# Neighbourhood heads: border keys by one transposition, meta keys by one product on diagonal blocks

## The chip, the cores and the metric

The kernel runs on one core of a Trainium2 chip. The time is that of the device for one execution, in microseconds. Engines are named as in the profile: PE (TensorE), ACT (ScalarE), DVE (VectorE), POOL (GpSimd), SP (SyncE, which issues nearly all DMAs).

## The reference

Two encoder layers over 512 grid tokens (8 rows of 64 columns) and 16 meta tokens, 1024 features, all in float32. Each layer projects the normed tokens into 42 chunks of 128 columns, runs two kinds of attention with 8 heads of 64, gates, projects and merges the results, and adds them to the residual. The part that matters here is the neighbourhood branch:

```python
s_mm = einsum('bqhd,bmhd->bhqm', qm, km) * scale                # meta queries see the meta keys alone
o_meta = einsum('bhqm,bmhd->bqhd', softmax(s_mm), vm)
...
s_win = einsum('bchd,bicjhd->bhcij', q_row, k_win) * scale      # a window of 8 rows x 16 columns
s_win = s_win + bias[None]
s_meta = einsum('bchd,bmhd->bhcm', q_row, km) * scale           # and the 16 meta keys
p = softmax(concatenate([s_win, s_meta], axis=-1))
return einsum('bhcij,bicjhd->bchd', p_win, v_win) + einsum('bhcm,bmhd->bchd', p_meta, vm)
```

## The kernel before, in words

**Precision.** A float32 operand x of a product is kept as a high part (x rounded to the matmul format F32R) and a low part (x minus the high part). Projections are three products per block of 128 rows: high by high, high by low, low by high (`product`, lines 387 to 397; tiles `whi`, `wlo` for weights, `hh`, `hl` for tokens). The helper `split` (lines 255 to 260) makes both parts from a bank of PSUM: ACT copies the high part, DVE subtracts. Weights come by DMA as `raw`, ACT casts them to `whi` (L306) and POOL subtracts for `wlo` (L307), three halves of a chunk ahead of their product. For the neighbourhood branch a product's 128 output rows are the 64 features by the high part of the values and the 64 features by their low part; `combine` adds the two halves (an ACT copy, then a DVE addition).

**Order of the work.** TensorE runs the projections without a break; attention is hung between them. After every half or whole chunk a `tick` runs what is due, for the neighbourhood heads (`side_na`) and for the other branch's heads (`side_gqa`; tiles S, av). A head's six stages (`windowed_head`, line 1029) are due 0, 2, 4, 5, 5 and 7 ticks after its start: load the bias, scores, transposes 1, 2 and 3, sums. The next head starts four ticks later at the earliest. The values of a pair of heads are transposed 3 and 4 ticks after the first head's start (`values`, `window_edges`). Each engine takes its instructions in one order, made by the scheduler from these places and from the table `BEHIND`, which names pairs of instructions of one engine that must follow each other (the n-th writer of a tile behind the m-th writer of another).

**One head.** Tokens stand column by column, so that 128 queries are 16 grid columns, and block b of queries needs a stretch of keys: 208, 272, 272 and 208 columns of an array of 544 (`BLK`), which holds the 512 keys and the 16 metas twice, behind key 63 and ahead of key 448. The four blocks of scores are two products each (Sb: keys' high and low parts). DVE adds the bias and takes the maximum (L1062), ACT takes the exponential into the bias tile (L1064). Then the weights of 128 keys are turned so that keys lie on partitions, by TensorE transpositions against an identity:

- ta (`transposes1`): four pieces of 128 keys; split into `tah`, `tal` of 512 columns.
- tb (`transposes2`): two pieces of 128 keys, and the two borders, each 64 border keys with 16 metas, 80 columns (block 0 to the left, block 3 to the right); split into `tbh`, `tbl`.
- tc (`transposes3`): 64 columns around the metas of blocks 1 and 2; a mask `inner` zeroes what isn't meta; the high parts go to rows 0 to 63 and the low parts to rows 64 to 127 of `na`, 256 columns (L864, L870).

`sums` (avb, L1124) is eleven products into one bank of 512 columns: one for `na` (256 columns), four for `tah` and `tal` and two for `tbh` and `tbl` (256), and four of 80 rows by 128 columns for the borders.

In layer 0 alone (`full`) the 16 meta queries have a softmax of their own: two products of 16 columns (sm), a transposition of a padded 128x32 tile (tm), a split by DVE into the padded tile `mm`, and a product of 16 columns (avbm).

The values tile `VB2` has six slots: 0 to 2 for inner keys, 3 and 4 for the borders with their metas (80 rows), 5 for the metas of blocks 1 and 2. `window_edges` fills 3 to 5 by three transpositions of 80 columns (vtc).

Of the kernel before, what the change touches and what calls it, by code (L numbers as in the profile page):

```python
# [18 lines left out]
P = 128  # L19
# [4 lines left out]
NMETA = 16  # L24
# [34 lines left out]
BLK = ((0, 0, 208), (480, 64, 272), (208, 208, 272), (752, 336, 208))  # L59
# [3 lines left out]
BLK_META = 448  # L63
# [10 lines left out]
    ),  # L74
    "DVE": (
# [7 lines left out]
    ),  # L83
# [12 lines left out]
    ),  # L96
    "Pool": (
        ("KB1_20", 0, "za1_0", 0), ("ga0", 7, "wlo0_24_0", 0), ("ga0", 51, "wlo1_36_1", 0), ("ga0", 52, "wlo1_36_1", 0),
        ("wl6KB", 1, "gb0", 0), ("wlo0_21_0", 0, "ga0", 10), ("wlo1_38_1", 0, "zb1_3", 0),
    ),  # L100
# [58 lines left out]
def trunk_kernel(ctx: ExitStack, tc: tile.TileContext, xT, w, gn, gf, bias, rope, out):  # L159
# [72 lines left out]
    for kind, (cols, n, dt) in {"ga": (256, 1, F32R), "na": (256, 1, F32R), "mm": (NMETA, 1, F32R), "pm": (32, 1, F32), "inv": (32, 1, F32)}.items():  # L232
# [9 lines left out]
    inner = cpool.tile([P, 1], F32, name="inner")  # L242
    nc.gpsimd.memset(inner, 1.0)
    nc.gpsimd.affine_select(inner, inner, pattern=[[0, 1]], compare_op=ALU.is_ge, fill=0.0, base=-NMETA, channel_multiplier=1)
    nc.gpsimd.affine_select(inner, inner, pattern=[[0, 1]], compare_op=ALU.is_ge, fill=0.0, base=3 * NMETA - 1, channel_multiplier=-1)

# [278 lines left out]
    for l in range(DEPTH):  # L525
# [74 lines left out]
        def stack_k(tag, name, k, n, eng):  # L600
# [6 lines left out]
            return [(t[:, 0], t[:, 1]) for t in (one, two_)]  # L607
# [85 lines left out]
        def pair_factors(t, c, n, name):  # L693

            f = slot("G", f"pf{name}{l}") if n > 1 else tiny.tile([P, P], F32, tag="pf", bufs=1, name=f"pf{name}{l}")
# [82 lines left out]
        def window_scaled(c, name):  # L778

            t, e = slots.tile([P, NKEY], F32, tag="E", bufs=BUFS["E"], name=name), HD + 2 * NMETA  # L780
            for ps, a, b in project(c, True):
                r = rbc[:, a:b]
                if a == 0:
                    nc.vector.tensor_mul(t[:, :HD], ps[:, :HD], r[:, :HD])
                    nc.vector.tensor_mul(t[:, e + HD:e + b], ps[:, HD:], r[:, HD:])
                else:
                    i, j = NREAL - HD - a, NREAL - a
                    nc.vector.tensor_mul(t[:, e + a:], ps[:, :i], r[:, :i])
                    nc.vector.tensor_mul(t[:, e:e + HD], ps[:, i:j], r[:, i:j])
                    nc.vector.tensor_mul(t[:, HD:e].rearrange("p (i t) -> p i t", i=2),  # L790
                                         ps[:, j:].unsqueeze(1).to_broadcast([P, 2, NMETA]),
                                         r[:, j:].unsqueeze(1).to_broadcast([P, 2, NMETA]))
            return t
# [13 lines left out]
        def window_edges(v, out, name):  # L807

            ps = bank(ps_t, f"vt{name}", "tp")
            for i, a in enumerate((0, EDGE, HD - NMETA)):  # L810
                nc.tensor.transpose(ps[:EDGE, P * i:P * (i + 1)], v[:, a:a + EDGE], ident)
            split(out[:EDGE, 3:, :, 0], out[:EDGE, 3:, :, 1], ps[:EDGE, :3 * P].rearrange("p (t h d) -> p t h d", t=3, h=2))
            nc.scalar.copy(out[HD:, 5], out[:HD, 5].bitcast(F32))
# [23 lines left out]
        def combine(tag, o, hh, av, c0, n):  # L837

            r, q = rows(hh)
            t = slot(tag, f"cmb{nc.next_id()}")  # L840
# [547 lines left out]
```

## Time and profile before

| what | value |
|---|---|
| median of 3 timed runs | 819.68 us (819.6 to 820.24) |
| the profiled execution's own time | 818.64 us |
| its span, first to last instruction | 816.7 us |
| granted clock of TensorE | 0.999 |
| neighbourhood heads | 16, eight in each layer |
| ta, tb, tc, tm, vtc transpositions | 64, 64, 16, 8, 24 |
| avb, sm, avbm products | 176, 16, 8 |

In the profile a row of a group has line, engine, operation, output and inputs, shapes, count, then the busy time, the mean of one in ns and the idle time of the engine ahead of them with what ended it. A row of the timeline has start and duration in us. A matmul's duration holds its latency, which overlaps the next one's, so durations of neighbours add up to more than the time between their starts. PEld is the loading of stationary weights, which runs beside the matmuls. A few matmul records can be missing.

### The profile page before, as it was taken

The numbers are of one execution on the slowest core, as the hardware profiler recorded it, in microseconds if no ns is written. First come the engines' busy times: TensorE is split into PE (matmuls) and PEld (weight loads), VectorE is DVE, ScalarE is ACT, GpSimd is POOL, SyncE is SP. The second block draws the span as 40 slices with busy tenths as digits, with TensorE's granted clock in tenths as the row PEclk, the third lists the DMA queues.
The fourth block names the chain that finished last, engine by engine and source line by source line (L and its number), as shares of the span: only waits on it lengthen the run. The fifth ranks groups of instructions, "written<-read, shape, count | busy, mean of one in ns | idle before, by whom it ended". The sixth has DMA issues, their size and how long they took to land.

```text
span 816.7 us, 16071 instructions
## 1 busy us (share of the span) xinstructions
PE 808.8 (99%) x5658; PEld 755.1 (92%) x5658; DVE 505.2 (62%) x1154; ACT 473.5 (58%) x1137; POOL 418.0 (51%) x362
## 2 busy tenths in 40 slices
PE   9999999999999999999999999999999999999997
PEld 9999999999999999999988989998988888888786
DVE  7566767796785662365547666676867655324733
ACT  8645777677865654443445557666758755544322
POOL 1654454454554544655754645554625555556651
PEclk9999999999999999999999999999999999999999
DMA  8347474667645563435555575766775555652602
GB/s 299 108 133 216 145 212 131 183 212 204 184 146 183 159 210 119 142 105 173 153 122 137 141 231 154 213 162 179 194 227 159 171 181 152 198 174 90 206 1 104
DMA packets 113248, 134.99 MB, mean 165 GB/s; under 512 B 31888, under 2 KB 66192, under 8 KB 113168
## 3 DMA queue, kind: packets, MB, share of 16 engines
q1 hardware_dynamic: 112448, 132.90, 54.9%
q8 instruction: 45, 0.74, 0.4%
q10 hardware_dynamic: 720, 1.06, 0.4%
q14 instruction: 35, 0.29, 0.1%
HBM read 98.50 MB, written 21.84 MB: 147 GB/s over the span
## 4 chain that ended last, share of the span: by engine, by line
PE 94%; DMA 2%; ACT 1%; DVE 1%; issue 1%; SPq 1%; POOLq 0%; POOL 0%; DVEq 0%; ACTq 0%
PE pp L393 20%; PE pp L391 20%; PE pp L392 20%; PE av L977 4%; PE y L393 4%; PE y L391 4%; PE y L392 4%; PE avb L1124 2%; PE S L627 2%; PE S L628 2%; PE pf L1306 2%; PE pf L1308 2%; PE pf L1307 2%; PE pp L516 2%; DMA raw<-in_w_dram 1%; PE Sb L628 1%
## 5 line engine op out<-in xcount | busy, mean ns | idle before, releaser
L307 POOL TENSOR_TENSOR wlo<-raw,whi 128x512 fp32r<-128x512 f32 x210 | 284.4, 1364 | 287.1 <-ACT whi L306 223.3
L391 PE MATMUL pp<-hh,whi 128*128 128x256 f32 (+2 forms) x1040 | 325.2, 313 | 0.0
L393 PE MATMUL pp<-hh,wlo 128*128 128x256 f32 (+2 forms) x1040 | 324.1, 312 | 0.0
L392 PE MATMUL pp<-hl,whi 128*128 128x256 f32 (+2 forms) x1040 | 323.4, 311 | 0.0
L393 PEld LDWEIGHTS pp<-hh,wlo 128*128 128x128 f32 x1040 | 195.7, 188 | 10.3
L392 PEld LDWEIGHTS pp<-hl,whi 128*128 128x128 f32 x1040 | 195.7, 188 | 9.3
L391 PEld LDWEIGHTS pp<-hh,whi 128*128 128x128 f32 x1040 | 195.9, 188 | 8.7
L306 ACT CAST whi<-raw 128x512 fp32r<-128x512 f32 x210 | 128.0, 619 | 106.3 <-PE pp L392 36.2
L970 POOL TENSOR_TENSOR ga<-pm,ga 32x128 fp32r<-32x128 f32 x64 | 39.4, 615 | 64.1 <-ACT ga L968 39.9
L939 DVE STREAM_TRANSPOSE P<-P 128x512 f32<-128x512 f32 x64 | 46.5, 727 | 29.8 <-ACT P L913 29.4
L1203 DVE TENSOR_TENSOR mg<-pp,rbc 128x256 f32<-128x256 f32 (+2 forms) x48 | 24.8, 516 | 54.0 <-PE pp L393 53.7
L909 DVE CUSTOM_DVE_ANT_0 P<-S,r 128x528 f32<-128x528 f32 x64 | 44.8, 701 | 15.5 <-PE S L628 14.7
L260 DVE TENSOR_TENSOR ptl<-P,pth 128x512 fp32r<-128x512 f32 x64 | 48.9, 780 | 4.7 <-ACT pth L259 4.2
L913 ACT ACTIVATE P<-P,st 128x528 f32<-128x528 f32 x64 | 47.2, 737 | 1.7
L1064 ACT ACTIVATE bias<-bias,stb 128x208 f32<-128x208 f32 (+1 forms) x64 | 31.0, 485 | 18.2 <-DVE stb L1062 18.2
L1204 ACT ACTIVATE mg<-mg 128x256 f32<-128x256 f32 (+2 forms) x48 | 23.6, 492 | 28.0 <-DVE mg L1203 27.9
L259 ACT CAST pth<-P 128x512 fp32r<-128x512 f32 x64 | 39.3, 614 | 0.9 <-DMA P<-turn 0.8
L392 PE MATMUL pp<-mx,whi 128*128 128x272 f32 (+1 forms) x128 | 36.4, 285 | 0.0
L391 PE MATMUL pp<-mx,whi 128*128 128x272 f32 (+1 forms) x128 | 36.4, 285 | 0.0
L393 PE MATMUL pp<-mx,wlo 128*128 128x272 f32 (+1 forms) x128 | 36.4, 285 | 0.0
L912 ACT ACTIVATE st<-st 128x1 f32<-128x1 f32 x64 | 12.9, 202 | 40.4 <-DVE st L909 40.1
L977 PE MATMUL av<-pth,VA 128*128 128x256 f32 x128 | 34.0, 289 | 0.0
(534 smaller groups left out, 1717.9 us busy)
## 6 DMA issues: line engine op xcount, KB each, us to landing
raw<-in_w_dram SPq DMA_DIRECT2D x210, 256.0 KB
turn<-P SPq DMA_DIRECT2D x32, 528.0 KB
P<-turn SPq DMA_DIRECT2D x128, 128.0 KB
bias<-in_bias_dram SPq DMA_DIRECT2D x16, 480.0 KB
KB<-KB SPq DMA_DIRECT2D x24, 272.0 KB
rawl<-in_w_dram SPq DMA_DIRECT2D x16, 256.0 KB
x<-in_xT_dram SPq DMA_DIRECT2D x8, 264.0 KB
xr<-in_xT_dram SPq DMA_DIRECT2D x8, 264.0 KB
```

The lines of the kernel that those rows point to most:

```text
L259: split_at["hi"] = nc.scalar.copy(hi, src)
L260: split_at["any"] = nc.vector.tensor_sub(lo, src, hi.bitcast(F32))
L306: cast = nc.scalar.copy(hi, raw)
L307: sub = nc.gpsimd.tensor_sub(lo, raw, hi.bitcast(F32))
L391: nc.tensor.matmul(ps, wh, rh[:, a:b], start=i == 0, stop=False)
L392: nc.tensor.matmul(ps, wh, rl[:, a:b], start=False, stop=False)
L393: nc.tensor.matmul(ps, wl, rh[:, a:b], start=False, stop=i == n - 1)
L909: newest["max"] = nc.vector.tensor_tensor_reduce(p[:n], joined(S)[:n], scale[:n].to_broadcast([n, NTOK]), 1.0, -3e38, ALU.mult, ALU.max, s ...
L913: nc.scalar.activation(p[:n], p[:n], AF.Exp, bias=st[:n, 1:2], scale=1.0, accum_out=st[:n, 2:3] if total is None else total)
L939: nc.vector.transpose(c["both"][:n, a:b], c["both"][:n, a:b])
L970: nc.gpsimd.tensor_sub(tm[64 + 32 * t:96 + 32 * t, n * t:n * (t + 1)], m, tm[:32, :n].bitcast(F32))
L977: nc.tensor.matmul(c["av"], rows2(c["t"][i][0]), c["t"][i][1], start=i == 0, stop=i == 8)
```

## The change: what it does

All of it is in the neighbourhood heads, their values, and the table.

- **Borders.** The four blocks change places in the bias tile (`BLK`), so that the last 64 keys of block 3 and the first 64 of block 0 lie side by side at column 416 (`ENDS`). One transposition of 128 columns turns both. From each, ACT copies the high part to its own 64 rows of a tile `ne`, and DVE writes the low part to the other 64 rows; one product contracts over both, 128 rows by 128 columns, against a values slot that holds the same 64 values twice.
- **Metas.** POOL copies the metas of all four blocks, each twice, into a tile `nm` of 128 columns; one transposition (tc) turns them. ACT multiplies by `sign` (minus one for the first 16 of every 32 rows, plus one for the others) into `nh`, rounded; DVE forms tp * `second` - `nh`, which is the high part in the first 16 rows and the low part in the others, and writes the 32 rows of a block to its own 128 columns of `na`, now 128x512. One product of 512 columns, against values that repeat the metas eight times, covers the metas of all four blocks. It is the seventh of nine products.
- **Meta queries (layer 0).** One sm product of 32 columns (the keys' high and low parts side by side), added by ACT and DVE; the probabilities are stored twice in a 16x32 tile, whose transposition moves 16 columns in the tc bank; avbm contracts over 32 rows.
- **Values.** `window_edges` does two transpositions of 128 columns; three copies and three subtractions fill the slots, two copies double the borders. `window_scaled` writes the metas to a tile of their own.
- **The table** `BEHIND` has 119 pairs; two of its lines are shown.

```diff
-BLK = ((0, 0, 208), (480, 64, 272), (208, 208, 272), (752, 336, 208))
+BLK = ((480, 0, 208), (0, 64, 272), (688, 208, 272), (272, 336, 208))
-BLK_META = 448
+ENDS, META_OF = 416, (1, 3, 0, 2)
...
-        ("tc0_0", 0, "pp0_19_0", 15), ("tc0_5", 0, "av0_3_0", 0), ("tc0_6", 0, "Sb0_7", 7), ("tm0_2", 0, "pp0_12_0", 0),
+        ("tc0_2", 0, "pp0_12_0", 3), ("tc0_2", 1, "Sb0_3", 1), ("tc0_2", 1, "Sb0_3", 2), ("tc0_4", 1, "av0_2_1", 7),
...
+            ps, (v, m) = bank(ps_t, f"vt{name}", "tp"), v
+            nc.tensor.transpose(ps[:, :P], v[:, NKEY - P:], ident)
+            nc.tensor.transpose(ps[:, P:2 * P], m, ident)
...
+        def split_meta(tp, name):
+            n, c = tp.partition_size(), tp.free_size()
+            hi = tiny.tile([P, P], F32R, tag="nh", bufs=1, name=f"nh{name}")[:, :c]
+            t = tiny.tile([32, c], F32R, tag="nq", bufs=1, name=f"nq{name}") if n == 32 else pad_tile("na")
             with tc.high_priority():
+                nc.scalar.mul(hi[:n], tp, sign[:n])
+                for g, r in enumerate(range(0, n, 32)):
+                    r, b = slice(r, r + 32), META_OF[g] if n > 32 else 0
+                    nc.vector.scalar_tensor_tensor(t[r, c * b:c * b + c], tp[r], second[r], hi[r].bitcast(F32), op0=ALU.mult, op1=ALU.subtract)
+            return t
...
+                with tc.high_priority():
+                    for i in range(2):
+                        nc.gpsimd.tensor_copy(c["nm"].rearrange("p (i j d t) -> p i j d t", i=2, j=2, d=2)[:, :, :, i], metas)
...
-                transposed(tp[:EDGE, 2 * P:3 * P], pb[0][:, :EDGE])
-                transposed(tp[:EDGE, 3 * P:4 * P], pb[3][:, P:P + EDGE])
+                transposed(tp[:, 2 * P:3 * P], c["bias"][:, ENDS:ENDS + P])
...
-                seq = [(5, c["m"], 0, 128, 384)]
+                seq = []
                 for t in c["a"]:
                     seq += [(0, t, 0, 0, 256), (1, t, 256, 128, 384)]
                 for t in c["b"]:
-                    seq += [(2, t, 0, 256, 512), (3, t, 256, 0, 128), (4, t, 384, 384, 512)]
+                    seq += [(2, t, 0, 256, 512)]
+                seq += [(3, c["e"][1], 0, 0, 128), (4, c["e"][0], 0, 384, 512)]
...
+                todo.insert(6, (VB2[:, 5, hh], c["m"], 0, 512))
```

The sums of head 1 in layer 1 on TensorE, before (avb is their bank, VB the values, the row's last entry the rows and columns moved):

```order
L1124 MATMUL avb_1_7666<-na_118,VB_0_7201 128x256
L1124 MATMUL avb_1_7666<-tah_1_7518,VB_0_7201 128x256 x2
L1124 MATMUL avb_1_7666<-tal_1_7519,VB_0_7201 128x256 x2
L1124 MATMUL avb_1_7666<-tbh_1_7579,VB_0_7201 128x256
L1124 MATMUL avb_1_7666<-tbh_1_7579,VB_0_7201 128x128 x2
L1124 MATMUL avb_1_7666<-tbl_1_7580,VB_0_7201 128x256
L1124 MATMUL avb_1_7666<-tbl_1_7580,VB_0_7201 128x128 x2
```

And the same sums now:

```order
L1141 MATMUL avb_1_7752<-tah_1_7601,VB_0_7276 128x256 x2
L1141 MATMUL avb_1_7752<-tal_1_7602,VB_0_7276 128x256 x2
L1141 MATMUL avb_1_7752<-tb_1_7661,VB_0_7276 128x256 x2
L1141 MATMUL avb_1_7752<-na_118,VB_0_7276 128x512
L1141 MATMUL avb_1_7752<-ne_1_7662,VB_0_7276 128x128 x2
```

Two of the short products are gone, and the metas' product went from the front to the seventh place and from 256 to 512 columns.

The border and meta transpositions of head 3 in layer 1 on TensorE, before, with the projection that follows (pp_8_0 is its bank, S the other branch's scores):

```order
L196 MATMUL tb_3_8244<-ident,bias_3_7946 128x128 x2
L196 MATMUL tb_3_8244<-ident,bias_3_7946 80x128 x2
L196 MATMUL tc_3_8255<-ident,bias_3_7946 64x128
L627 MATMUL S_3_0_0_8267<-KA1h_6924,Q_1_6601 128x256
L628 MATMUL S_3_0_0_8267<-KA1l_6925,Q_1_6601 128x256
L627 MATMUL S_3_0_0_8267<-KA1h_6924,Q_1_6601 128x272
L628 MATMUL S_3_0_0_8267<-KA1l_6925,Q_1_6601 128x272
L391 MATMUL pp_8_0_8291<-hh_0_5821,whi_8_0_8163 128x512
```

And the same place now, from the border group on:

```order
L203 MATMUL tb_3_8339<-ident,bias_3_8037 128x128 x3
L635 MATMUL S_3_0_0_8365<-KA1h_6996,Q_1_6673 128x256
L636 MATMUL S_3_0_0_8365<-KA1l_6997,Q_1_6673 128x256
L635 MATMUL S_3_0_0_8365<-KA1h_6996,Q_1_6673 128x272
L636 MATMUL S_3_0_0_8365<-KA1l_6997,Q_1_6673 128x272
L399 MATMUL pp_8_0_8389<-hh_0_5893,whi_8_0_8258 128x512
L400 MATMUL pp_8_0_8389<-hl_0_5894,whi_8_0_8258 128x512
L401 MATMUL pp_8_0_8389<-hh_0_5893,wlo_8_0_8259 128x512
L399 MATMUL pp_8_0_8389<-hh_1_5967,whi_8_0_8258 128x512
L400 MATMUL pp_8_0_8389<-hl_1_5968,whi_8_0_8258 128x512
L401 MATMUL pp_8_0_8389<-hh_1_5967,wlo_8_0_8259 128x512
L399 MATMUL pp_8_0_8389<-hh_2_6042,whi_8_0_8258 128x512
```

And one row further down (hl_2 by whi stands between):

```order
L401 MATMUL pp_8_0_8389<-hh_2_6042,wlo_8_0_8259 128x512
L399 MATMUL pp_8_0_8389<-hh_3_6117,whi_8_0_8258 128x512
L400 MATMUL pp_8_0_8389<-hl_3_6118,whi_8_0_8258 128x512
L203 MATMUL tc_3_8351<-ident,nm_3_8171 128x128
L401 MATMUL pp_8_0_8389<-hh_3_6117,wlo_8_0_8259 128x512
```

tc reads nm in place of the bias tile, and it moved behind the scores and eleven products of the next projection.

On POOL, for the same head, now (wlo is a half chunk's low part, its numbers are the chunk and the half; ga belongs to the other branch):

```order
L315 TENSOR_TENSOR wlo_24_1_8123<-raw_24_1_7992,whi_24_1_8122 128x512
L315 TENSOR_TENSOR wlo_8_0_8259<-raw_8_0_7998,whi_8_0_8258 128x512
L1079 COPY nm_3_8171<-bias_3_8037 128x4x16 x2
L978 TENSOR_TENSOR ga_116<-pm_2_0_8063,ga_116 32x128 x2
L315 TENSOR_TENSOR wlo_8_1_8265<-raw_8_1_8114,whi_8_1_8264 128x512
```

The two copies stand behind the first half of the chunk in whose products tc now stands, and ahead of its second half.

More of the change, by code (lines that the diff above doesn't have):

```diff
@@ L231, in trunk_kernel @@
     padded = {}
-    for kind, (cols, n, dt) in {"ga": (256, 1, F32R), "na": (256, 1, F32R), "mm": (NMETA, 1, F32R), "pm": (32, 1, F32), "inv": (32, 1, F32)}.items():
+    for kind, (cols, n, dt) in {"ga": (256, 1, F32R), "na": (NREAL, 1, F32R), "inv": (32, 1, F32)}.items():
         padded[kind] = deque(cpool.tile([P, cols], dt, name=f"{kind}{i}") for i in range(n))
@@ L239, in pad_tile @@
         return padded[kind][0]
[L242 to L245, printed above, removed]
+    second, sign = (cpool.tile([P, 1], F32, name=n) for n in ("second", "sign"))
+    nc.gpsimd.memset(second, 1.0)
+    for r in range(0, P, 32):
+        nc.gpsimd.affine_select(second[r:r + 32], second[r:r + 32], pattern=[[0, 1]], compare_op=ALU.is_ge, fill=0.0, base=-NMETA,
+                                channel_multiplier=1)
+    nc.gpsimd.tensor_scalar(sign, second, 2.0, -1.0, op0=ALU.mult, op1=ALU.add)
     x1d = dpool.tile([NREAL, D], F32, name="x1d")
@@ L606, in stack_k @@
                 nc.sync.dma_start(t[to].bitcast(F32), one[r].bitcast(F32))
-            return [(t[:, 0], t[:, 1]) for t in (one, two_)]
+            return [(t[:, 0], t[:, 1], t) for t in (one, two_)]
         def stack_soon(tag, name, k, n, hh):
@@ L807, in window_edges @@
         def window_edges(v, out, name):
[L809 to L813, printed above, removed]
+            ps, (v, m) = bank(ps_t, f"vt{name}", "tp"), v
+            nc.tensor.transpose(ps[:, :P], v[:, NKEY - P:], ident)
+            nc.tensor.transpose(ps[:, P:2 * P], m, ident)
+            src = ps[:, :2 * P].rearrange("p (t h d) -> p t h d", t=2, h=2)
+            parts = [(out[HD * i:HD * i + HD, 4 - i], src[HD * i:HD * i + HD, 0]) for i in range(2)] + [(out[:, 5], src[:, 1])]
+            with tc.high_priority():
+                for t, p in parts:
+                    nc.scalar.copy(t[:, :, 0], p)
+                for t, p in parts:
+                    nc.vector.tensor_sub(t[:, :, 1], p, t[:, :, 0].bitcast(F32))
+            nc.scalar.copy(out[HD:, 4], out[:HD, 4].bitcast(F32))
+            nc.scalar.copy(out[:HD, 3], out[HD:, 3].bitcast(F32))
         v = scaled(VA, f"va{l}")
@@ L1099, in transposes2 @@
                 transposed(tp[:, P:2 * P], pb[3][:, 0:P])
-                transposed(tp[:EDGE, 2 * P:3 * P], pb[0][:, :EDGE])
-                transposed(tp[:EDGE, 3 * P:4 * P], pb[3][:, P:P + EDGE])
-                c["b"] = bh, bl = slot("B", f"tbh{nm}", F32R), slot("B", f"tbl{nm}", F32R)
-                split(bh[:, :256], bl[:, :256], tp[:, :256])
-                split(bh[:EDGE, 256:512], bl[:EDGE, 256:512], tp[:EDGE, 256:512])
+                transposed(tp[:, 2 * P:3 * P], c["bias"][:, ENDS:ENDS + P])
+                t, e = slot("B", f"tb{nm}", F32R), slot("B", f"ne{nm}", F32R)
+                c["b"] = t[:, :256], t[:, 256:512]
+                c["e"] = e[:, :P], e[:, P:2 * P]
+                ends = list(zip((rows(0), rows(1)), c["e"]))
+                with tc.high_priority():
+                    nc.scalar.copy(c["b"][0], tp[:, :256])
+                    for (r, o), t in ends:
+                        nc.scalar.copy(t[r], tp[r, 2 * P:3 * P])
+                    nc.vector.tensor_sub(c["b"][1], tp[:, :256], c["b"][0].bitcast(F32))
+                    for (r, o), t in ends:
+                        nc.vector.tensor_sub(t[o], tp[r, 2 * P:3 * P], t[r].bitcast(F32))
             def transposes3():
                 tp = bank(ps_t, f"tc{nm}", "tp")
-                transposed(tp[:64, :P], c["bias"][:, BLK_META:BLK_META + 64])
-                c["m"] = tm = pad_tile("na")
-                split_meta([(tm[:, P:2 * P], tp[:, :P]), (tm[:, :P], tp[:, :P])], inner)
+                transposed(tp[:, :P], c["nm"])
+                c["m"] = split_meta(tp[:, :P], nm)
+                if full:
+                    transposed(tp[:32, P:P + NMETA], c["pm"], NMETA)
+                    c["mt"] = split_meta(tp[:32, P:P + NMETA], nm)
             def sums():
@@ L1119, in sums @@
                 for t in c["b"]:
-                    seq += [(2, t, 0, 256, 512), (3, t, 256, 0, 128), (4, t, 384, 384, 512)]
-                for i, (u, t, c0, a, b) in enumerate(seq):
-                    r = slice(0, EDGE if u in (3, 4) else P)
-                    nc.tensor.matmul(av[:, a:b], rows2(VB2[r, u, hh]), t[r, c0:c0 + b - a], start=i == 0,
-                                     stop=i == len(seq) - 1, skip_group_check=True)
+                    seq += [(2, t, 0, 256, 512)]
+                seq += [(3, c["e"][1], 0, 0, 128), (4, c["e"][0], 0, 384, 512)]
+                todo = [(VB2[:, u, hh], t[:, c0:c0 + b - a], a, b) for u, t, c0, a, b in seq]
+                todo.insert(6, (VB2[:, 5, hh], c["m"], 0, 512))
+                for i, (v, t, a, b) in enumerate(todo):
+                    nc.tensor.matmul(av[:, a:b], rows2(v), t, start=i == 0, stop=i == len(todo) - 1, skip_group_check=True)
                 def collect(av=av):
@@ L1134, in sums @@
                     c["avm"] = bank(ps_t, f"avbm{nm}", "tp")[:, :NMETA]
-                    nc.tensor.matmul(c["avm"], rows2(VB2[:, 5, hh]), c["mt"], start=True, stop=True)
+                    nc.tensor.matmul(c["avm"], rows2(VB2[:32, 5, hh]), c["mt"][:32], start=True, stop=True)
                 ending.append(collect)
@@ L1158, in window_values @@
                 kvq[j]["o"] = slot("B", f"ob{l}_{j}")
-                values(vb, kvq[j]["v2"], [(t, P * t + 2 * EDGE, P) for t in range(3)], f"b{l}_{j}")
+                values(vb[0], kvq[j]["v2"], [(t, P * t + 2 * NMETA, P) for t in range(3)], f"b{l}_{j}")
             else:
```

70 lines of the change are left out of this document (26 added, 44 removed), and 59 rows, old and new, of the table BEHIND.

## The prediction

> **What bounds the kernel now.** I read the page's head first, then the chain of waits, then the list of who TensorE waited for, and last its timeline around one head.
>
> ```profile
> span 816.7 us, 16071 instructions
> PE 808.8 (99%) x5658; PEld 755.1 (92%) x5658; DVE 505.2 (62%) x1154; ACT 473.5 (58%) x1137; POOL 418.0 (51%) x362
> PEclk9999999999999999999999999999999999999999
> PE 94%; DMA 2%; ACT 1%; DVE 1%; issue 1%; SPq 1%; POOLq 0%; POOL 0%; DVEq 0%; ACTq 0%
> ```
>
> TensorE is busy 808.8 of 816.7 us at the full granted clock, and the chain that ended last runs through it for 94%. A busy TensorE need not be at its peak, so the second question is whether it ever stands still for others. All its waits:
>
> ```profile
> PE warm L203 <- PEq L1376: 0.8, 1, 0.8
> PE S L627 <- DVE stb L1062: 0.8, 1, 0.8
> PE pp L516 <- DVE hh L408: 0.2, 1, 0.2
> PE avb L1124 <- DVE na L870: 0.2, 1, 0.2
> PE av L977 <- DVE ptl L260: 0.2, 1, 0.2
> ```
>
> That is 2.2 us, of which 1.2 (S, avb, av) lie among the heads. So the time is the sum of what TensorE's instructions hold it for, one after the other, and an instruction taken from its queue shortens the end by its own hold unless a new wait appears. The hold is not the duration in the groups (a matmul's latency overlaps the next), but the distance between starts.
>
> **The change part by part.** *Transpositions.* A head's border group, the metas' transposition behind it and the scores product that follows (start, duration):
>
> ```profile
> 495.90 0.60 PE L196 MATMUL tb<-ident,bias 128*128 128x128 f32 x4
> 496.33 0.27 PE L196 MATMUL tc<-ident,bias 128*64 128x128 f32 x1
> 496.36 0.36 PE L627 MATMUL S<-KA1h,Q 128*128 128x256 f32 x1
> 496.56 0.28 PE L628 MATMUL S<-KA1l,Q 128*128 128x256 f32 x1
> 496.68 0.29 PE L627 MATMUL S<-KA1h,Q 128*128 128x272 f32 x1
> ```
>
> Four tb transpositions hold it from 495.90 to 496.33, 0.108 us each. The last of a row seems to cost 0.03, but the first product behind it then takes 0.20 where the next takes 0.12: 0.03 + 0.08, again 0.11. The old border pair has 80 stationary columns and costs no less than a full one, so going from two of 80 to one of 128 saves one whole hold: 16 heads x 0.108 = 1.7 us. The border values of a pair of heads go from three transpositions to two, priced by the same row: 8 x 0.108 = 0.9 us.
>
> *The weighted sum.* Products of 512 columns, then the eleven products of one head, then the next projection:
>
> ```profile
> 503.20 0.40 PE L391 MATMUL pp<-hh,whi 128*128 128x512 f32 x1
> 503.44 0.39 PE L392 MATMUL pp<-hl,whi 128*128 128x512 f32 x1
> 503.67 0.40 PE L393 MATMUL pp<-hh,wlo 128*128 128x512 f32 x1
> 503.90 0.28 PE L1124 MATMUL avb<-na,VB 128*128 128x256 f32 x1
> 504.02 0.41 PE L1124 MATMUL avb<-tah,VB 128*128 128x256 f32 x2
> 504.26 0.40 PE L1124 MATMUL avb<-tal,VB 128*128 128x256 f32 x2
> 504.50 0.46 PE L1124 MATMUL avb<-tbh,VB 128*128 128x256 f32 x3
> 504.79 0.51 PE L1124 MATMUL avb<-tbl,VB 128*128 128x256 f32 x3
> 505.13 0.33 PE L391 MATMUL pp<-hh,whi 128*128 128x256 f32 x1
> 505.30 0.28 PE L392 MATMUL pp<-hl,whi 128*128 128x256 f32 x1
> ```
>
> A product of 512 columns holds TensorE 0.23 us, one of 256 columns 0.12 (five from 503.90 to 504.50). The eleven take 505.13 - 503.90 = 1.23 plus 0.05 by which the product behind them is held up (0.17 for 0.12): 1.28. Seven of 256 are 0.84, so the four of 128 columns cost 0.44, 0.11 each: twice what their columns suggest, since something that doesn't shrink with the columns sets their distance. The new nine are six of 256, one of 512 and two of 128: 0.72 + 0.23 + 0.22 = 1.17. Both versions move 2304 columns; the gain is only in the two short products, less what the column count gives back. 16 x 0.11 = 1.8 us.
>
> The Trainium skill, "TensorE: Matmul & The Clock Gate", section "Back-to-back issue gap", gives sustained spacings of 81 ns for 128 columns and 131 ns for 512. By it two short products would save 0.16 and the long one cost 0.01 more than the 0.12 of the one it replaces, 2.4 us in all. The rows above disagree with it at both sizes (0.11 and 0.23), and the sum goes by them.
>
> *The meta queries of layer 0* (8 heads). Two score products of 16 columns fall to one of 32; one transposition (tm) keeps its 32 stationary columns and moves 16 in place of 128; their own weighted product (avbm) contracts over 32 rows in place of 128. Nearest rows: the score products, and the meta queries' sums of the other branch, which move 64 columns against 128 stationary ones:
>
> ```profile
> 114.92 0.17 PE L627 MATMUL sm<-KB,QB_1a 128*16 128x16 f32 x1
> 114.94 0.17 PE L628 MATMUL sm<-KB,QB_1a 128*16 128x16 f32 x1
> 114.97 0.28 PE L977 MATMUL avm<-pthm,VA 128*128 128x64 f32 x1
> 115.08 0.28 PE L977 MATMUL avm<-ptlm,VA 128*128 128x64 f32 x1
> ```
>
> One sm product less is 0.03: 8 x 0.03 = 0.2 us. The small transposition lies between 0.03 (sm) and 0.11 (tc above); it has few columns on both sides, as sm has, so I take 0.03, and 8 x 0.08 = 0.6 us is saved; at the other end nothing. The avbm product keeps 128 stationary columns, as avm has at 0.11, and the 80-row products above cost 0.11 as well, so I book no gain for fewer rows; if it fell to sm's 0.03, 0.6 us more.
>
> *Sum on TensorE*: 1.7 + 0.9 + 1.8 + 0.2 + 0.6 = 5.2 us from 64 instructions fewer. The profiled execution took 818.64 us, 1.94 us of it outside the span, and is 1.04 us below the median of the three timed runs, 819.68. The saving is taken off the median: 814.5.
>
> *What is added elsewhere.* VectorE has 64 small subtractions of the metas where there were 32, and 32 half-height border subtractions for 16 of 80 rows; ScalarE has 48 instructions more (32 border copies for 16, three copies of border values for one and a second duplicate, the small softmax). GpSimd gets 32 copies of 128x64 (nm). Prices:
>
> ```profile
> L870 DVE SCALAR_TENSOR_TENSOR na<-tc,inner,na 32x128 fp32r<-32x128 f32 x32 | 11.0, 344 | 1.8 <-ACT na L864 1.2
> L260 DVE TENSOR_TENSOR tbl<-tb,tbh 80x256 fp32r<-80x256 f32 x16 | 6.7, 419 | 2.6 <-ACT tbh L259 2.5
> L259 ACT CAST tbh<-tb 80x256 fp32r<-80x256 f32 x16 | 5.9, 367 | 0.5 <-DVE tbl L260 0.2
> L307 POOL TENSOR_TENSOR wlo<-raw,whi 128x512 fp32r<-128x512 f32 x210 | 284.4, 1364 | 287.1 <-ACT whi L306 223.3 <-PE pp L393 8.8 <-PE pp L392 8.5
> L970 POOL TENSOR_TENSOR ga<-pmm,ga 32x64 fp32r<-32x64 f32 x2 | 0.6, 320 | 1.0 <-ACT ga L968 0.9
> L644 POOL COPY qmt<-q 128x16 f32<-128x16 f32 x4 | 1.2, 320 | 1.4 <-DVE q L573 1.4
> ```
>
> VectorE: 32 x 0.34 + 16 x 0.42 = 18 us at most, to about 64% of the span; ScalarE: 48 x 0.37 = 18 us at most, to about 60%. GpSimd: a copy lies between 0.32 (qmt, ga) and 1.36 (wlo, eight times the columns); estimate 0.4 by the nearer two, so 13 us, to 53%. No engine comes near TensorE, so this costs nothing as long as each result is there when TensorE comes to it. The cover is the distance between a head's scores and the transposition of its metas:
>
> ```profile
> 483.69 0.26 PE L627 MATMUL Sb<-KB,QB_0a 128*128 128x208 f32 x1
> ```
>
> From 483.69 to the tc row at 496.33 lie 12.6 us. In it now fall four score reductions, four exponentials and, new, the two copies. ScalarE, VectorE and GpSimd keep these in their queues behind other work, and whatever stands behind tc on TensorE's queue, the projections, would wait too. The edited table puts tc later in several heads of the second layer; the metas' product moves from first to seventh of its sum, so the wait on na (0.2 us now) gets 0.7 us of cover. The further copies of border values stand three ticks of the head's clock before the first sum that reads them. SP's queue has the same 692 entries, partly in another order.
>
> **The rivals.** *Half the gain is given back*: more and later evacuations make TensorE wait a little at many heads, for a bank of PSUM or for tb, ne or na. For: the waits above are of this kind and VectorE has the longest list of additions. Against: 1.2 us in 16 heads is little. At 0.2 us (the size of those waits) per head, 16 x 0.2 = 3.2 us: 817.7.
>
> *Slower: GpSimd's queue decides.* nm stands behind wlo subtractions, and wlo waits 223.3 us in all for ScalarE's whi, which waits for buffers that TensorE frees. If the copies of three heads come 3 us after TensorE reaches tc, 9 us are lost: 819.68 - 5.2 + 9 = 823.5. It decides from 5.2 us, 0.33 per head. For: GpSimd's long idle times are spent inside such waits. Against: the list of TensorE's waits has no GpSimd row; the order shows nm right behind a wlo that TensorE needs before tc anyway; 12.6 us of lead.
>
> *Nothing to gain*: the weights' loads set the pace, and TensorE only waits elsewhere: 819.7. Against: DMA is 2% of the chain. For: the chain has such pieces at all, and they would grow if TensorE ran ahead.
>
> **How the numbers follow.** Forecast, 814.5: 0.67; its own range is 812.7 (avbm's 0.6 and the 1.2 us of waits gone too) to 816 (the small transposition at 0.11 and about 1 us of new waits). Half given back, 817.7: 0.18. Nothing to gain, 819.7: 0.08. Slower, 823.5: 0.07. Leaving out the last two (0.15), the range is 812.7 to 817.8. About 0.2%, 1.6 us, is what a measurement of this kernel can tell from no change, so faster means below 818.0: the first two cases, 0.85; within it 0.08; slower 0.07.
>
> **What would show it.** Right: 5594 TensorE instructions for 5658; three tb rows 0.108 apart; avb's nine within 1.17 us; TensorE's waits still near 2 us; the span near 811.5. The half case shows as many waits of tc, avb or tb on VectorE or ScalarE. The slower one shows tc waiting for GpSimd nm, in the second layer above all. The prediction is wrong if the 512-column product holds TensorE clearly longer than 0.23 us, or if DMA's share of the chain grows by the 5 us.

## The result, and the profile after

The change made the kernel slower: 825.24 us, median of 6 runs (824.62 to 826.6), against 819.77 us for the kernel before in the same job (6 runs). The ratio is 1.0064 with a 95% interval of 1.0051 to 1.0077. The forecast was 814.5 us, the range 812.7 to 817.8: off by 10.7 us, and on the other side.

The profiled execution took 825.65 us, 7.0 us over that of before. Its page's head:

```profile
span 823.9 us, 16123 instructions
PE 812.8 (99%) x5594; PEld 752.1 (91%) x5594; DVE 525.4 (64%) x1210; ACT 477.3 (58%) x1185; POOL 427.3 (52%) x395
PE 93%; DVE 2%; issue 2%; ACT 1%; POOL 0%; DMA 0%; POOLq 0%; SPq 0%; ACTq 0%; DVEq 0%
```

TensorE has 64 instructions fewer, as forecast, VectorE's 64% is the one of the working and GpSimd's 52% is near it, and yet the span grew by 7.2 us, at the same granted clock (0.999 in both profiles). The changed stage does in detail what the forecast said. The first head of layer 1 on TensorE's timeline, its border group and then its sums:

```profile
504.53 0.49 PE L203 MATMUL tb<-ident,bias 128*128 128x128 f32 x3
504.86 0.27 PE L203 MATMUL tc<-ident,nm 128*128 128x128 f32 x1
...
512.50 0.40 PE L1141 MATMUL avb<-tah,VB 128*128 128x256 f32 x2
...
513.21 0.40 PE L1141 MATMUL avb<-na,VB 128*128 128x512 f32 x1
513.45 0.33 PE L1141 MATMUL avb<-ne,VB 128*128 128x128 f32 x2
513.62 0.33 PE L399 MATMUL pp<-hh,whi 128*128 128x256 f32 x1
513.79 0.28 PE L400 MATMUL pp<-hl,whi 128*128 128x256 f32 x1
```

Three tb transpositions hold TensorE 0.33 us, 0.11 each. The nine products hold it from 512.50 to 513.62, and the one behind them is 0.05 late (0.17 for 0.12): 1.17 us, the forecast to the hundredth. The 512-column product holds it 0.24. The Trainium skill, "TensorE: Matmul & The Clock Gate", section "Back-to-back issue gap", gives 131 ns for it; this trace doesn't agree, and the measurement decides.

So where is the time? The first product on the merged tokens (mx) follows the last head of layer 0, and the last product of all ends layer 1. Both in before:

```profile
370.28 0.28 PE L391 MATMUL pp<-mx,whi 128*128 128x256 f32 x1
...
810.59 0.28 PE L1308 MATMUL pf<-wl15h,mx 128*128 128x256 f32 x1
```

The same two after:

```profile
379.02 0.28 PE L399 MATMUL pp<-mx,whi 128*128 128x256 f32 x1
...
817.84 0.28 PE L1324 MATMUL pf<-wl15h,mx 128*128 128x256 f32 x1
```

Layer 0 is 8.7 us longer, layer 1 is 1.5 us shorter (810.59 - 370.28 = 440.31 against 438.82). What TensorE waited for, after:

```profile
PE tb L203 <- DVE tal L268: 1.2, 1, 1.2
PE tc L203 <- DVE VB L824: 1.0, 1, 1.0
```

With seven more of 0.2 to 0.8 us the list makes 5.0 us, 2.8 more than before, out of 7.2. The rest must be in the distances between instructions that wait for nobody. Layer 0 alone has the meta queries, so I looked there. The end of a layer-0 head's sums, with the meta queries' product avbm:

```profile
103.10 0.39 PE L1141 MATMUL avb<-na,VB 128*128 128x512 f32 x1
103.33 0.33 PE L1141 MATMUL avb<-ne,VB 128*128 128x128 f32 x2
103.59 0.27 PE L1151 MATMUL avbm<-nq,VB 32*128 32x16 f32 x1
103.79 0.38 PE L635 MATMUL S<-KA0h,Q 128*128 128x256 f32 x1
104.02 0.28 PE L636 MATMUL S<-KA0l,Q 128*128 128x256 f32 x1
```

Two ne products need 0.17 us in layer 1; here avbm starts 0.26 behind the first, and what follows it another 0.20 later. The product of 32 rows, booked at nothing, is surrounded by gaps.

### The profile page after: what moved, and what is told of

It reads as the page before. It is cut to its first block, busy times and chain, and to the rows that moved or that the text cites. A ratio compares the mean times of both kernels' runs of the same rounds, so it can differ in the third digit from the quotient of the medians.

```text
span 823.9 us, 16123 instructions
## 1 busy us (share of the span) xinstructions
PE 812.8 (99%) x5594; PEld 752.1 (91%) x5594; DVE 525.4 (64%) x1210; ACT 477.3 (58%) x1185; POOL 427.3 (52%) x395
## 4 chain that ended last, share of the span: by engine, by line
PE 93%; DVE 2%; issue 2%; ACT 1%; POOL 0%; DMA 0%; POOLq 0%; SPq 0%; ACTq 0%; DVEq 0%
PE pp L401 20%; PE pp L399 20%; PE pp L400 20%; PE av L985 4%; PE y L401 4%; PE y L399 4%; PE y L400 4%; PE avb L1141 2%; PE S L635 2%; PE S L636 2%; PE pp L524 2%; PE pf L1324 2%; PE pf L1322 2%; PE pf L1323 2%; PE Sb L636 1%
## 5 line engine op out<-in xcount | busy, mean ns | idle before, releaser
L978 POOL TENSOR_TENSOR ga<-pm,ga 32x128 fp32r<-32x128 f32 x64 | 42.6, 666 | 85.1 <-ACT ga L976 49.7
L985 PE MATMUL av<-ptl,VA 128*128 128x256 f32 x128 | 33.7, 287 | 0.3 <-DVE ptl L268 0.3
```

The costliest lines, as they stand in the source:

```text
L978: nc.gpsimd.tensor_sub(tm[64 + 32 * t:96 + 32 * t, n * t:n * (t + 1)], m, tm[:32, :n].bitcast(F32))
L985: nc.tensor.matmul(c["av"], rows2(c["t"][i][0]), c["t"][i][1], start=i == 0, stop=i == 8)
```

## The experiments

Four questions, in the order in which they arose. All medians stand against before's runs of the same job (819.0 to 819.9 us); ratios have 95% intervals. Where a text says that an order is kept, every engine's queue is written out in full in place of the table `BEHIND`; the traces show the same instructions in the same order.

### 1. Do short row counts hold TensorE, or is it the table?

**Padded to 128 rows.** The changed kernel, whole computation, with both short tiles (pm, 16 rows; nq, 32 rows) padded to 128:

```diff
-            t = tiny.tile([32, c], F32R, tag="nq", ...) if n == 32 else pad_tile("na")
+            t = pad_tile("nq" if n == 32 else "na")
-    transposed(tp[:32, P:P + NMETA], c["pm"], NMETA)
+    transposed(tp[:32, P:2 * P], c["pm"])
-    ... rows2(VB2[:32, 5, hh]), c["mt"][:32] ...
+    ... rows2(VB2[:, 5, hh]), c["mt"] ...
```

> The changed kernel with the meta queries' two small instructions on all 128 rows again: the probabilities lie in a padded 128x32 tile whose transposition moves 128 columns, and their weighted product contracts over 128 rows, of which 96 are zeros. The order of every engine's instructions is held as in the changed kernel. Theory A (a stationary of 32 rows or fewer between products of 128 rows holds TensorE 0.3 to 0.4 us in place of 0.11, in 16 places): 825.2 - 8 x 0.29 - 8 x 0.20 = 821.3 us, between 820.5 and 822. Rival B (the row count costs nothing, the whole loss is late evacuations): 825.2, not under 824.5.

Measured: 820.18 us, 1.0011 [1.0002, 1.002], a little below theory A's range. Against the change's 1.0064 that is 0.53%, 4.3 us, from two operations per head in 8 heads. The same place as above:

```profile
102.63 0.40 PE L1105 MATMUL avb<-na,VB 128*128 128x512 f32 x1
102.86 0.34 PE L1105 MATMUL avb<-ne,VB 128*128 128x128 f32 x2
103.03 0.23 PE L1115 MATMUL avbm<-nq,VB 128*128 128x16 f32 x1
103.11 0.36 PE L599 MATMUL S<-KA0h,Q 128*128 128x256 f32 x1
103.32 0.28 PE L600 MATMUL S<-KA0l,Q 128*128 128x256 f32 x1
```

From na to the second S product: 0.69 us against 0.92, so 0.23 per head. The transposition, first in the change (16 rows), then padded:

```profile
97.00 0.26 PE L635 MATMUL Sb<-KB,QB_0b 128*128 128x208 f32 x1
97.18 0.18 PE L203 MATMUL tc<-ident,pm 16*32 16x16 f32 x1
97.30 0.36 PE L636 MATMUL Sb<-KB,QB_0b 128*128 128x208 f32 x1
97.50 0.31 PE L635 MATMUL Sb<-KB,QB_0b 128*128 128x272 f32 x1
```

```profile
96.70 0.26 PE L599 MATMUL Sb<-KB,QB_0b 128*128 128x208 f32 x1
96.80 0.27 PE L167 MATMUL tc<-ident,pm 128*32 128x128 f32 x1
96.83 0.34 PE L600 MATMUL Sb<-KB,QB_0b 128*128 128x208 f32 x1
97.01 0.31 PE L599 MATMUL Sb<-KB,QB_0b 128*128 128x272 f32 x1
```

0.50 us against 0.31: the smaller transposition holds TensorE 0.19 longer. Together 8 x (0.23 + 0.19) = 3.4 us of the 4.3; the list of waits also loses its 1.2 and its 1.0.

**Each short operation alone, in the kernel before**: tm's input cut to 16 rows by 16 columns, `c["pm"][:NMETA]` (whole computation); avbm contracting over 32 rows, `VB2[:32, 5, hh]` with `c["mt"][:32]`; over 64 rows; and two such products of 32 rows one behind the other. The last three leave out the low part of the meta queries' probabilities, which before's `mm` holds in rows 64 to 95.

> The kernel before with one edit: the meta queries' probabilities are transposed from their 16 rows alone, moving 16 columns, where it was 128 rows and 128 columns; every engine's order is held as before. Same output. Theory A: 8 x 0.20 = 1.6 us longer, 821.3. Rival B, as the prediction had it: 8 x 0.08 = 0.6 us shorter, 819.1.

Measured: 821.31 us, 1.0022 [1.0013, 1.0031].

> The kernel before with one edit: the meta queries' weighted product contracts over the first 32 rows in place of 128, which leaves out the low part of their probabilities; every engine's order is held as before. Theory A: 8 x 0.29 = 2.3 us longer, 822.0. Rival B, as the prediction had it: 819.7, at most 0.6 us shorter.

Measured: 821.0 us, 1.0023 [1.0011, 1.0034].

> Before, in its own order, with only the meta queries' weighted product over the first 64 rows in place of 128 (leaves out the low part of their probabilities). With 32 rows this cost 1.7 us in 8 heads. If every product of fewer than 128 rows in a changed row split pays for entering and leaving, 821 us as with 32 rows; if only 32 rows pay, 819.4 us, no change.

Measured: 820.98 us, 1.0025 [1.0014, 1.0036].

> Before in its own order, the meta queries' weighted product over 32 rows (as in e3, 821.0 us, leaves out the low part of their probabilities) and directly behind it a second product of the same 32 rows, whose result nobody reads. If what costs is entering and leaving the 32-row shape, the second product is nearly free: 8 x 0.03 to 0.1, 821.2 to 821.8 us. If each 32-row product costs its own 0.2 to 0.3 us, 823 us.

Measured: 821.85 us, 1.0036 [1.0024, 1.0048]. With nothing else changed, one short operation costs 1.8 to 2.0 us in 8 heads, 0.22 to 0.26 each, and two in a row 3.0 us. From 64 rows nothing is gained over 32. The timelines with 64 rows, and with two products of 32 rows:

```profile
102.98 0.27 PE L1106 MATMUL avbm<-mm,VB 64*128 64x16 f32 x1
103.18 0.38 PE L598 MATMUL S<-KA0h,Q 128*128 128x256 f32 x1
```

```profile
102.69 0.38 PE L1108 MATMUL avbm<-mm,VB 32*128 32x16 f32 x2
103.01 0.38 PE L598 MATMUL S<-KA0h,Q 128*128 128x256 f32 x1
```

From avbm to the S product it is 0.20 us with one, 0.32 with two: the second costs 0.12, about the 0.11 of a full-height product of few columns. What costs is going from 128 rows to 64 or fewer and back, once each, whatever stands in between. The Trainium skill, "TensorEngine Tiling (Array Packing)", section "Key Properties", says that changing the tiling mode drains TensorE. For the number of rows these runs agree, and price the pair of changes at about 0.23 us. A change of columns alone, from 128*128 to the 128*32 of the padded turn above, shows no more than an ordinary hold. Nor does every number of rows under 128 cost: before's two border products of 80 rows stand between products of 128, and tbh holds TensorE 0.29 us in the rows of the prediction (504.50 to 504.79), 0.12 for its 256 columns and 0.17 for the two. After, the two ne products of 128 rows take the same 0.17 (513.45 to 513.62).

**Without the table.** The change with `BEHIND = {}`, whole computation:

> The changed kernel with the table of pairs emptied, so that the scheduler alone sets the order. Theory A leaves about 7 us of waits in layer 0 to explain. If the table puts VectorE's evacuations late there (theory C), the time without it is shorter than 825.2, near 821 to 823. If the waits come with the added work on VectorE and ScalarE and the table only eases them (rival D), it is longer, 828 to 835.

Measured: 863.51 us, 1.0543 [1.0524, 1.0562], far outside what either theory expected. So order carries about 5% in this kernel. That doesn't show that the new table is worse than the old: it says how much a bad order can cost, and led to the next question.

### 2. Is it the order of the queues?

The padded kernel still has 5.7 us more than the forecast. I moved single instructions of ACT, DVE and POOL to other places in their queues, so that what TensorE was seen to wait for came earlier, in the padded kernel, the change, and before as a yardstick of what such moves bring anywhere; then a second time, on a model of the queues made from the traces. All do the whole computation. A control writes before's own order out in full.

```diff
-BEHIND = {...}
+ORDER = """..."""    # every engine's queue in full, the moved instructions in their new places
```

> The padded version of the change (820.18 us) with the same instructions, and only the queue order of ScalarE (65 of 1043 places), VectorE (74 of 1061) and GpSimd (2) changed at 38 points, where TensorE waited for evacuations in the trace of the padded version; TensorE's own order is kept. In that trace TensorE has 27 waits of more than 0.03 us on another engine, 5.2 us together (before: 6, 1.05 us). Theory 'order': the added evacuations fit beside TensorE, they only stand at wrong places of the queues; then about 4 us of these waits and of the 0.1 us behind each go, 814.7 to 817 us. Rival 'work': the added copies and subtractions themselves are what TensorE waits for, and whatever is moved ahead delays something else that is waited for: 818.7 us or more.

> The changed kernel as it is (products over 32 and 16 rows stay), with its queue order changed by the same procedure at 50 points (ScalarE 79 places, VectorE 73, GpSimd 5). Theory 'order': 825.2 us falls by about 5 us to 819 to 821, still 4 to 5 us above e5, which is the price of the short products. Rival 'work': 823.5 us or more.

> The kernel before with its queue order changed by the same procedure, which finds only 7 points (VectorE 23 places, ScalarE 10), since TensorE has 6 waits on other engines there, 1.05 us. Theory 'order': about 0.9 us less than before, 818.5 us. Rival 'work' says the same; this run is the yardstick: if it falls by 3 us or more, the order was no better in before than in the changed kernel, and the comparison of e5 with before would be unfair.

> The padded version of the change again, TensorE's, SyncE's order as in the changed kernel; ScalarE (138 of 1043 places), VectorE (77 of 1061) and GpSimd (6) in another order, found on a model of the queues that has the durations, the spacings and the semaphores of the traces so far (the first reordering had only the data dependences, and won about 0.9 us after 190 us but lost 2.7 us before). Nothing ahead of 90 us is moved. By the model 7.3 us less than the padded version, and since the model was up to 3 us off: theory 'order' (the added work fits beside TensorE) 813 to 817 us; rival 'work' (it does not fit, waits come back elsewhere) 819 us or more.

> The changed kernel with its short products as they are, reordered with the same means (ScalarE 113 of 1043 places, VectorE 105 of 1061). Theory 'order': 7.8 us less by the model, 816 to 819 us, and 2 to 5 us above e9, the price of the products over 32 and 16 rows. Rival 'work': 822 us or more.

> The kernel before, reordered with the same means (ScalarE 46 of 995 places, VectorE 55 of 1013). By the model 1.9 us less than before: 817.5 us by both theories. It is the yardstick of e9: if e9 is under this by 3 us or more, the removed instructions are worth about what was forecast (5.2 us less the small turn's 0.6), and the loss of the changed kernel is short products and order alone.

> Control: the kernel before, the same instructions in the same order on every engine, only that the order is written out in full in place of the table's pairs, as in e2, e3, e8 and e12. Both theories of the short products need 819.3 us here. If it is 821, the 1.7 us of e2, e3 and e8 would come from the writing out and not from the short products.

| kernel | as it was | first order | second order |
|---|---|---|---|
| padded | 820.18; 1.0011 [1.0002, 1.002] | 821.14; 1.0022 [1.0013, 1.0031] | 821.51; 1.003 [1.002, 1.0041] |
| the change | 825.24; 1.0064 [1.0051, 1.0077] | 824.7; 1.0064 [1.0051, 1.0078] | 825.69; 1.0077 [1.0065, 1.0089] |
| before | 1 | 821.63; 1.003 [1.002, 1.004] | 822.12; 1.0042 [1.0028, 1.0055] |

The control gave 819.21, 0.9994 [0.9984, 1.0003]. No order made anything clearly faster; the expected 814 to 817 for the padded kernel was far off, and so was the yardstick, since before lost 2.5 and 3.4 us by the same procedure where it was to win 1 and 2. So these moves cost time of their own. In the first order the padded kernel ends 0.5 us below before in its first order, in the second 0.6 us below before in its second, by the medians, not the 3 us that would show the forecast gain. A wait that a move took away came back elsewhere, as in the first order of before, where a step of the border values now stood ahead of a key's low part:

```profile
PE S L605 <- DVE KA0l L595: 2.0, 1, 2.0
```

The theory isn't borne out. It isn't excluded either: two attempts are few, with a procedure that made before slower too.

### 3. Is it the added work on VectorE?

The padded kernel with less to do, its order written out. First, one of the four meta subtractions per head instead of four, the border's high part copied once for both halves and its low part not formed (this leaves work out):

```diff
-                for g, r in enumerate(range(0, n, 32)):
+                for g, r in enumerate(range(0, min(n, 32), 32)):
...
+                c["e"] = e[:, :P], e[:, :P]
...
+                    nc.scalar.copy(e[:, :P], tp[:, 2 * P:3 * P])
```

> The padded version of the change, its order kept, with 80 VectorE and 16 ScalarE instructions left out (leaves out three of the four parts of each head's meta weights, and the low parts of the borders, whose two half-height copies become one). TensorE's instructions stay. Theory 'work on VectorE': most of the 4 to 5 us of added waits go, 815.5 to 817.5 us. Theory 'order': the waits for ob, ga, ptl, whi and wlo stay, only those for na, ne and nq go (1 us), 819 us or more.

Measured: 817.14 us, 0.9967 [0.9955, 0.9978], below before, which no other kernel so far clearly was: 0.44%, 3.6 us, less than the padded one.

Then the first line alone, the meta subtractions without the border part (leaves work out):

> The padded version of the change (820.2 us), its order kept, with three of the four 32-row VectorE subtractions of each head's metas left out (leaves out three of the four parts of the meta weights); the borders stay as they are. If the metas' subtractions are the load, near e14: 817 to 818.3 us. If the borders' halves are, 819.3 to 820.2 us.

Measured: 818.4 us, 0.9991 [0.9982, 1.0]: 0.20%, 1.6 us less than the padded one, for 48 subtractions of 0.35 us in layers 0 and 1; the value lies just outside what was expected if the metas are the load. The border part with its 16 ScalarE copies is the other 2.0 us; no run has it alone. Why so much, on an engine that idles a third of the time? The stretch from 60 to 290 us, which lies in the heads of layer 0, by engine; first before, then the padded kernel, then the one with less vector work:

```profile
60.00:290.00 230.00, 230.00 (x1922) 229.61 (x1922) 166.05 (x451) 156.40 (x426) 115.42 (x103) 1.00 0.61 180
```

```profile
60.00:290.00 230.00, 228.29 (x1862) 224.64 (x1861) 172.99 (x475) 159.11 (x460) 115.14 (x117) 1.00 0.60 177
```

```profile
60.00:290.00 230.00, 228.80 (x1880) 226.38 (x1879) 160.51 (x437) 158.31 (x453) 118.01 (x119) 1.00 0.61 179
```

The columns are PE, PEld, DVE, ACT, POOL, with the number of instructions. In this stretch VectorE was busy 72% before (166.05 of 230) where its share of the span is 62%, and TensorE's record had no gap at all. In the padded kernel VectorE has 7 us more and TensorE 1.7 us of gaps; with less vector work 1.2. So VectorE's load isn't all of it: in the last kernel it is below before's (160.51 against 166.05), and gaps remain. The gaps in the record are the small part: most pauses (summed below) are shorter than a product's latency and leave TensorE's record closed. Where such a queue gets late, in the change, VectorE and then GpSimd from 213.6 us on:

```profile
214.24 1.80 DVE L862 TENSOR_TENSOR ob<-ob,zb 128x528 f32<-128x528 f32 x1
...
216.67 0.69 DVE L268 TENSOR_TENSOR tal<-ta,tah 128x512 fp32r<-128x512 f32 x1
217.63 1.81 DVE L268 TENSOR_TENSOR ob<-ob,ob 128x528 fp32r<-128x528 f32 x1
```

```profile
214.03 1.45 POOL L315 TENSOR_TENSOR wlo<-raw,whi 128x512 fp32r<-128x512 f32 x1 [2.21 <-ACT whi L314]
...
217.59 1.28 POOL L315 TENSOR_TENSOR wlo<-raw,whi 128x512 fp32r<-128x512 f32 x1 [2.12 <-ACT whi L314]
```

And TensorE there, which waits for that tal and then for the VB subtractions, since each holds a bank of PSUM until it is done:

```profile
217.51 0.41 PE L203 MATMUL tb<-ident,bias 128*128 128x128 f32 x2 [1.22 <-DVE tal L268]
```

The wait for VB, 1.0 us in the list above, follows at 220.76. Two VectorE operations take 1.80 us each; both started just behind a GpSimd subtraction (214.24 behind 214.03, 217.63 behind 217.59). In the padded kernel the first of them starts together with GpSimd's:

```profile
211.86 0.70 DVE L826 TENSOR_TENSOR ob<-ob,zb 128x528 f32<-128x528 f32 x1
```

```profile
211.85 1.86 POOL L279 TENSOR_TENSOR wlo<-raw,whi 128x512 fp32r<-128x512 f32 x1 [2.21 <-DMA raw<-in_w_dram]
```

There VectorE takes 0.70 us for the same operation, and GpSimd's is the longer one. The Trainium skill, "GPSIMD Engine Reference", section 1, lists GpSimd's SBUF interfaces as shared with VectorE, with contention for instructions of two SBUF inputs. These rows agree: the one that started later grew, by 1.1 us in the change. So the price of lateness is uneven: a step that comes just behind a GpSimd subtraction grows by about 1 us, and TensorE waits for the ones behind it, while one that comes first doesn't grow.

Two things limit the reading. The padded kernel has all the added vector work, and neither of these two waits: the rows show what a late queue costs, not that the added work alone makes it late. And order alone moved before by up to 3.4 us, so the 1.6 us of the subtractions aren't clear of such accidents, and the 3.6 us of both omissions barely are.

### 4. Is it GpSimd's copies?

The rival of the prediction. The padded kernel without the two copies of nm (leaves work out: the metas are zeros); both omissions together; and the whole computation with the four meta subtractions made one on VectorE, and the four placements given to GpSimd:

```diff
-                c["nm"] = tiny.tile([P, P], F32, tag="nm", ...)
+                c["nm"] = pad_tile("zn")
...
-                        nc.gpsimd.tensor_copy(c["nm"]...)
...
+                nc.vector.scalar_tensor_tensor(hi[:n], tp, second[:n], hi[:n].bitcast(F32), ...)
+                for g, b in enumerate(META_OF):
+                    ...
+                    nc.gpsimd.tensor_copy(t[r, c * b:c * b + c], hi[r]...)
```

> The padded version of the change, its order kept, without the 32 GpSimd copies that gather the metas (the transposition reads a tile of zeros; leaves out the metas of the real queries). GpSimd's copies take 0.24 us each, and VectorE instructions of two operands run up to 1.1 us longer beside GpSimd's work. Theory 'GpSimd in the way': 817 to 818.5 us. Theories 'work on VectorE' and 'order': 819.7 to 820.2 us, next to nothing.

Measured: 821.51 us, 1.0021 [1.0012, 1.003], slower than with the copies and outside what was expected.

> Both left out. If the added work is all that the forecast of the padded version missed, this comes near what TensorE's sum gives, 819.3 - 4.6 = 814.7 us: 814.7 to 817 us. Theory 'order': 818.5 us or more.

Measured: 818.92 us, 0.9985 [0.9976, 0.9993]: not the 814.7 to 817 us of the added work, but the 818.5 or more of theory 'order'.

> The whole computation: one VectorE subtraction of 128 rows per head, and four GpSimd copies of 32 x 128 that put it on the diagonal (64 more GpSimd copies at about 0.3 us, 19 us of its 48% idle time). Theory 'work on VectorE': as e17 plus what GpSimd's copies cost by coming later, 817.5 to 819.5 us, under before's 819.3 if they are well placed. If VectorE beside GpSimd is slowed as much as it is relieved, 820 us or more.

Measured: 820.06 us, 1.0015 [1.0006, 1.0024]. The copies aren't the cause: leaving them out gains nothing, with or without the vector work. Why does it lose 0.8 and 1.5 us against the padded kernel and the one with less vector work? The trace without the copies has one new wait, 0.9 us, on a low part (ptl) of the other branch:

```profile
170.84 0.39 PE L949 MATMUL av<-ptl,VA 128*128 128x256 f32 x1 [0.91 <-DVE ptl L232]
```

```profile
169.09 1.70 DVE L232 TENSOR_TENSOR ptl<-P,pth 128x512 fp32r<-128x512 f32 x1
```

```profile
168.95 1.29 POOL L279 TENSOR_TENSOR wlo<-raw,whi 128x512 fp32r<-128x512 f32 x1
```

With the copies GpSimd waited in front of them until 173.5 us, and this ptl took 0.68 us; without them it starts its subtraction 0.14 us ahead of ptl, which takes 1.70. The kernel with both omissions has the same wait, 0.8 us. It is the collision of question 3 once more. The last one takes 48 operations off VectorE, gives GpSimd 64, and ends level with the padded kernel: another wait came, on GpSimd.

```profile
PE av L955 <- POOL ga L948: 1.2, 1, 1.2
```

No kernel that does the whole computation beats before.

## Why the prediction was wrong, point by point

To size the terms I summed, for each kernel, the usual distance of starts (the median over the five kernels together) over all pairs of neighbouring TensorE instructions by line and shape (*hold*), and apart from it whatever a pair took over that by more than 0.05 us (*pause*):

| kernel | hold, us | pauses | in all, us |
|---|---|---|---|
| before | 799.0 | 105 | 10.3 |
| the change | 797.6 | 152 | 18.4 |
| padded | 794.4 | 150 | 16.1 |
| padded, less vector work | 794.4 | 133 | 13.8 |
| padded, one meta subtraction | 794.4 | 135 | 15.1 |

Only the differences are used: many pauses are in every kernel, as the late second product behind a row of transpositions. They depend somewhat on the grouping. With the instruction ahead of each pair taken into its group, over all twenty kernels, before has 3.8 us more hold than the padded kernel and the change 3.6 us, and the change's pauses are 6.8 us over before's. So a part is known to about 1 us.

- **The bound**: right. An instruction taken from TensorE's queue shortened the hold by its own.
- **Transpositions, values, sums, sm** (1.7 + 0.9 + 1.8 + 0.2 = 4.6 us): right as far as the sums can tell. Padded against before, 799.0 - 794.4 = 4.6; the rows above bear out the border group and the sums one by one.
- **The small transposition**, "I take 0.03, and 8 x 0.08 = 0.6 us is saved": wrong, and outside both its ends. It was priced by a product of few columns and 128 rows; it has 16 rows, and costs 0.19 more than the padded one, 1.5 us.
- **avbm**, "so I book no gain for fewer rows": the size was bounded on one side alone, between 0 and a gain of 0.6. It costs 8 x 0.23 = 1.8 us. The 80-row products of before, which I took as a sign that rows don't matter, are on the free side: 80 rows cost nothing extra, 64 do. The hold shows both small operations together as 797.6 - 794.4 = 3.2 us, the timelines as 3.4, the measured times as 4.3; in those are also the waits that went with the padding. The price could be read in before's own trace, which has five transpositions of 10 rows (mt) between products of 128:

```profile
47.27 0.28 PE L393 MATMUL pp<-hh,wlo 128*128 128x256 f32 x1
47.48 0.47 PE L709 MATMUL mt<-ident,msb 10*128 10x10 f32 x5
47.88 0.65 PE L800 MATMUL vta<-ident,va 128*128 128x128 f32 x4
```

From 47.27 to 47.88 are 0.61 us, where 0.12 for the product and five times 0.06, the distance of two neighbouring mt, would make 0.42: about 0.2 for going to few rows and back.
- **Added work**, "No engine comes near TensorE, so this costs nothing as long as each result is there when TensorE comes to it": the condition failed, and no price was set for that in the forecast itself. VectorE's 64% was a mean over the span, and the stage that matters stood at 72% already. "The cover" was measured for one path, the metas of a head; the banks of PSUM behind tal and the border values have no such cover, as the change's two longest waits show. Less vector and scalar work took 3.6 us back; that it was the lateness of VectorE which cost them is argued from the rows, not shown by itself.
- **The rivals.** *Half given back* named the mechanism, TensorE waiting for tb or tc's evacuations, at 3.2 us; the pauses grew by 8.1 (18.4 - 10.3), few of them long enough for the list of waits, so the size that it gave was less than half of that. *GpSimd's queue*: right sign, wrong mechanism; no wait of the change names nm, and its 823.5 is near the measured time by luck. *Nothing to gain*: no, DMA stays off the chain.

In sum, by the ratios: from the forecast (814.5 of 819.68, 0.9937) to the change (1.0064) is 1.27%, 10.4 us. Padding takes 4.3 of them, less vector work 3.6, each known to a little over 1 us by the intervals. The other 2.5 us stay open: 0.6 is the turn's saving that doesn't exist, and 1.9 lie among the pauses that are left (13.8 us against 10.3), for which no run names one cause.

## What to carry to other kernels

In a row of full products on TensorE, don't let a small one drop to 64 rows or fewer: padding it with zeros to 128 cost an ordinary hold here, the short one 0.2 us more; 80 rows cost nothing extra. Read the load of an engine in the stage that gets the new work, not over the span, and ask of each bank of PSUM which evacuation frees it and what now stands ahead of that. Look for a row of the same height in the whole trace, not only in the stage that changes; where a price has none, bound it on both sides of zero.

## What the runs showed of the hardware beyond that

A wait costs more than the list of waits says. The padded kernel on TensorE at 245 us:

```profile
245.03 0.29 PE L365 MATMUL y<-ob,wlo 128*128 128x272 f32 x1
245.58 0.39 PE L363 MATMUL pp<-hh,whi 128*128 128x256 f32 x1 [0.26 <-DVE mb L1189]
245.80 0.28 PE L364 MATMUL pp<-hl,whi 128*128 128x256 f32 x1
```

The list counts 0.26 us, from the end of the product ahead (245.32). But that product usually holds TensorE 0.13 us, and here the next starts 0.55 behind it; the one after that starts another 0.22 later, where 0.12 is usual. Together that is 0.42 + 0.10 = 0.52 us, twice what the list says, and a pause that ends before the product ahead does isn't in the list at all. So the prediction's check of TensorE's standstill by this list was too mild a one.
